# A two-layer hybrid transformer on one core: the experts' output gate computed earlier, and the order of the experts' weight loads

## The chip, the cores and the metric

The kernel runs as one program on one NeuronCore of a Trainium2 chip. The metric is the device time of one execution in microseconds (us). Every weight is read from HBM once per execution; the activations stay on the chip. The engines named below are PE (TensorE, matmuls), PEld (its weight loads, in the records), DVE (VectorE), ACT (ScalarE), POOL (GpSimd) and SP (SyncE, which here only issues weight loads).

## The reference

One sequence of 256 tokens, width 1024, two layers, all in f32:

```
for l in range(DEPTH):                       # DEPTH = 2
    mod = silu(c) @ w_ada[l] + b_ada[l]      # c: (1, 1024), w_ada[l]: (1024, 6144)
    sh1, sc1, g1, sh2, sc2, g2 = split(mod, 6)
    h = rms_norm(x, gain[l, 0]) * (1 + sc1) + sh1
    # four token mixers (NSA, sliding window, MoBA, MLA) read h @ w_in[l]
    mixed = sum_i(sigmoid(G_i h) * (mixer_i @ w_branch[l, i])) @ w_out[l]
    x = x + g1 * mixed
    h2 = rms_norm(x, gain[l, 1]) * (1 + sc2) + sh2
    x = x + g2 * hier_moe(h2, w_coarse, b_coarse, w_fine, b_fine, w13, w2)
```

`hier_moe` picks one of 4 groups and 2 of its 8 experts for each token; an expert is `(silu(a) * b) @ w2[e]` with `a, b = split(x @ w13[e], 2)`, `w13[e]` 1024x512 (2 MB) and `w2[e]` 256x1024 (1 MB). All 32 experts are read in each layer. The part of the change is `g2`, the gate on the experts' output: 1024 columns of `mod`, a product of a vector with a 4 MB slice of `w_ada[l]`.

## The kernel before, in words

**One layer.** A layer has two stages. In the first, the mixers, PE works through a list of *units* (projections, attention, gates, output projection), and beside it a *side list* of smaller units. A written-out string `SEQ[l]` says which list gives the next unit: a letter `a` takes the next one of the side list. The side list holds `ada(l, part)`, the slices of `mod` other than the experts' gate. In the second stage, `experts(l)`, the experts run in eight rounds p = 0..7 of four experts each, an expert's two halves of `w13` first, then its two halves of `w2`.

**The slice of mod.** `ada_pe(l, part)` (L554) makes five units of one slice and a last group. Units 0 to 3 are four matmuls each (32x512, `mm<-ring,cs` or `mm<-pg,cs` in the order; each shows as two records in the trace), each unit with one 1 MB load of `w_ada`. Unit 4, `evac`, copies the sum from PSUM by ACT to a tile `gt` and adds two bias rows by small DMAs on POOL. For part 5 two `rows` units follow, which spread the row over 128 partitions (one matmul and one ACT copy each). In `experts(l)` before, these seven units are called through `filler(n)`: unit 0 ahead of the last part of the router, units 1 to 3 and `evac` between that part and `route`, the two `rows` units in round p = 0 after `first(p, 1)`.

**The route.** `route` is a chain of small DVE instructions on the router's logits; PE continues behind it with short matmuls on `smb` with the constants `tri` and `one_b`, then the seeds (`mm<-pg,K`), the gather of tokens (`at<-pg 128x256`) and `first(0, 0)`, the first expert matmuls.

**The weights.** All weight loads go through SP's one queue in the order of `plan`. A load of 1 MB takes one of 8 slots of `ring`, or (tag "any") two pages of 0.5 MB where no ring slot is free; the halves of `w2`, 0.5 MB each, take one page and never a ring slot. `advance()` walks the plan while the program is built, and stops at the first load that finds no place; `done(key)` gives a place back and calls `advance()` again. On the chip each load waits for the last reader of the place that it takes, and all behind it in the queue wait too. In the plan before, the four loads of part 5 stand behind the loads of `w_out`, and directly ahead of the first `w13`.

In the rows, nearly all engine instructions stand at L253 (a helper that records each), the weight loads at L320 and the router's weights for the next layer at L415 and L416.

Of the kernel before, what the change touches and what calls it, by code (L numbers as in the profile page):

```python
# [49 lines left out]
def shape_constants():  # L50
# [20 lines left out]
    for b, sl in enumerate(_slopes()):  # L71
        for i in range(2):
# [8 lines left out]
SEQ = {0: "u u p u p u p u u u p f p u p f f p A f f q f A A p f f A A r f A N N N . p w f . p p p f . N N b N "  # L81
# [25 lines left out]
SEQ = {l: t.split() for l, t in SEQ.items()}  # L107

KEYS = {0: "in,0,0,1 in,0,0,0 in,0,1,0 in,0,1,1 in,0,2,0 ada,0,3,0 in,0,2,1 ada,0,3,2 ada,0,3,1 ada,0,3,3 "
# [10 lines left out]
KEYS = {l: [tuple(int(f) if f.isdigit() else f for f in k.split(",")) for k in t.split()] for l, t in KEYS.items()}  # L120
KREC = {}
REC = {}
# [136 lines left out]
def kernel(ctx, tc, x_in, c_in, w_ada, b_ada, norm_gain, w_in, qk_gain, cmp_pe, cmp_w1, cmp_w2,  # L259
# [36 lines left out]
    plan, tiles, free = [], {}, {"ring": NRING, "pg": 0}  # L296
    nxt = [0]

    def unit(key, *dmas, tag="ring"):
        plan.append((key, dmas, tag))  # L300

    def advance():
        while nxt[0] < len(plan):
            key, dmas, tag = plan[nxt[0]]
            if tag == "any":
                tag = "ring" if free["ring"] or free["pg"] < 2 else "pg"
            m = 2 if tag == "pg" and len(dmas) == 2 else 1
            if free[tag] < m:
                return
            free[tag] -= m  # L310
            if tag == "ring":
                t = [T_("ring", [128, 2048])]
            else:
                t = [pg([128, 1024]) for _ in range(m)]
            if len(t) == 1 and len(dmas[0]) == 5:
                dmas = [(0, 2048, dmas[0][2], dmas[0][4])]
            for i, d in enumerate(dmas):
                o0, o1, n, src = d[:4]
                d = t[0][:, o0:o1] if m == 1 else t[i]
                nc.sync.dma_start(d.rearrange("p (k n) -> p k n", n=n) if n else d, src)  # L320
            tiles[key] = t[0] if m == 1 else t
            M.t["D"] = max([M.t["D"]] + [M.free(a.tensor.name) for a in t]) + (1.5 if tag == "pg" and m == 1 else 2.9)
            for a in t:
                M.known(a, M.t["D"] + 2.0)
            nxt[0] += 1
# [1062 lines left out]
    def ada(l, part):  # L1388
        how = HOW[l][part]
        return ada_pe(l, part) if how == "p" else ada_v(l, part, how == "g")  # L1390


    def fill_list(l):
# [26 lines left out]
        out = u[0][:4] + [m[1]] + u[0][4:] + u[1][:2] + r[0:1] + u[1][2:4] + r[1:2] + u[1][4:8] + g[0:2]  # L1420
        out += u[2][:4] + r[2:3] + u[2][4:] + g[2:3]
        rbias = router_bias(l)
        if l == 0:
            rest = load_rest()
            side = [(None, lambda: next(rest, None), None, 0)] * LOADN
            side += ada(0, 3) + rbias + ada(0, 2) + ada(0, 4) + [(None, lambda: params(1), None, 0.1)] + ada(1, 1)
            side += [(None, lambda: V.tensor_copy(tri, tri_f), None, 0)]
        else:
            side = ada(1, 4) + ada(1, 3) + rbias + ada(1, 2)
        first = gemm_units(l, 0, CH[0][1], first_fin, ("uh", "ul")) + [(None, lambda: gate_tile(l), None, 0)]  # L1430
        loads = LOADN if l == 0 else 0
        every = (len(base) * LASTS[l] - SIDE[l]) / (len(side) - loads)
# [10 lines left out]
                keys.append(side[n][1][2])  # L1443
                n += 1
        keys += [x_[1][2] for x_ in side[n:]] + [x_[2] for x_ in out]
        return base + out, side, len(base) + 6, keys

    P1 = 2
    P2 = 2
# [8 lines left out]
    LASTS = (0.98, 0.98)  # L1458
    LOADS = 2.0
    LOADN = 8  # L1460
    fills = [fill_list(l) for l in range(DEPTH)]

    def expert(p, b, s):
# [3 lines left out]
    def plan_all():  # L1467
        seen = set()

        def add(key):  # L1470
            if key is not None and key not in seen:
                seen.add(key)
                plan_key(key)

        for k in range(4):
            add(("ada", 0, 1, k))
        for l in range(DEPTH):
            for k in range(2):
                add(("in", l, 0, k))
            for k in range(4):  # L1480
                add(("ada", l, 0, k))
            for key in (KEYS or {}).get(l) or fills[l][3]:
                add(key)
            for key in fills[l][3]:
                add(key)
            KREC[l] = [k for k in dict.fromkeys(fills[l][3]) if k]
            for k in range(4):
                add(("ada", l, 5, k))
            for p in range(NE // 4):
                for b in range(2):  # L1490
                    for hf in range(2):
                        for s in range(2):
                            add(("w13", l, expert(p, b, s), hf))
                for b in range(2):
                    for k in range(2):
                        for s in range(2):
                            add(("w2", l, expert(p, b, s), k))
# [5 lines left out]
    def mixers(l):  # L1503
# [61 lines left out]
            return True  # L1565

        free["pg"] = 0
        R.clear()
        OT.clear()
        M.reset()  # L1570
# [498 lines left out]
                                T.matmul(acc[t][n], st[:, 0, 128 * t:128 * t + 128], y[:, j], start=False, stop=False)  # L2069

    def experts(l):
        units = ada_pe(l, 5)

        def filler(n):
            for _ in range(n):
                units.pop(0)[1]()


        acc = {}

# [2 lines left out]
            for n in range(2):  # L2083
                T.matmul(acc[t][n], ID, X[t][:, 512 * n:512 * n + 512], start=True, stop=False)

        filler(1)
        mm = router_part(l, 3)
        seeds(0)
        rs = rstd_of(H["ss"])
# [11 lines left out]
                c = slice(512 * h, 512 * h + 512)  # L2101
                A.activation(H["hh"][t][:, c], X[t][:, c], AF.Copy, scale=rs[:, t:t + 1])
        mm()
        filler(4)
        most, further, weights = route(l, rs, lo)
        seeds(1)

# [3 lines left out]
        def prep_sel(q):  # L2111
            SEL[q], ST[q] = selection(rk[:, :, 4 * q:4 * q + 4], 4)
            XG[q] = [pg([128, 4, 256]) for _ in range(2)]
# [25 lines left out]
        def second(p, gT):  # L2139
# [12 lines left out]
                        done(("w2", l, expert(p, b, e), k))  # L2152
            return ys

        prep_sel(0)
        most()
        for i in range(1, 4):
# [8 lines left out]
        for p in range(NP):  # L2166
# [12 lines left out]
            h = first_half(h, masks(p)[0])  # L2179
            g = swiglu(first(p, 1), h, masks(p))  # L2180
            if p == 0:
                filler(2)
            if p:
                scatter(acc, ST[(p - 1) // 2][:, (p - 1) % 2], ys, False)
            if nxt:
# [82 lines left out]
```

## Time and profile before

| what | value |
|---|---|
| median of 3 runs | 1033.31 us (1030.22 to 1036.1) |
| the profiled execution's own time | 1038.59 us |
| its span | 1037.0 us |
| PE busy in the span | 982.9 us (95%), 5175 matmuls |
| DVE, ACT, POOL busy | 538.9, 406.5, 134.7 us |
| read from HBM | 335.36 MB |
| layer 0: first expert matmul | 309.26 us |
| layer 1: first expert matmul | 816.17 us |
| last record but the output | 1031.7 us |

The span runs from the first to the last instruction of the profiled execution; the execution's own time is 1.6 us longer, and lies 5.3 us above the median of the runs. All positions below are us from the span's start.

### The profile page before, as it was taken

The numbers are of one execution on the slowest core, as the hardware profiler recorded it, in microseconds if no ns is written. First come the engines' busy times: TensorE is split into PE (matmuls) and PEld (weight loads), VectorE is DVE, ScalarE is ACT, GpSimd is POOL, SyncE is SP. The second block draws the span as 40 slices with busy tenths as digits, with TensorE's granted clock in tenths as the row PEclk, the third lists the DMA queues.
The fourth block names the chain that finished last, engine by engine and source line by source line (L and its number), as shares of the span: only waits on it lengthen the run. The fifth ranks groups of instructions, "written<-read, shape, count | busy, mean of one in ns | idle before, by whom it ended". The sixth has DMA issues, their size and how long they took to land.

```text
span 1037.0 us, 14343 instructions
## 1 busy us (share of the span) xinstructions
PE 982.9 (95%) x5175; PEld 601.1 (58%) x5176; DVE 538.9 (52%) x1237; ACT 406.5 (39%) x997; POOL 134.7 (13%) x271
## 2 busy tenths in 40 slices
PE   5999999999999999998899989999999999999996
PEld 2667777777774444442346857777878444444332
DVE  1667678979772222221156865987785523222112
ACT  1564857674442111110146557677354221111111
POOL 0031346302000000000001341603200000000000
PEclk7999999999999999999999989999999999999999
DMA  9977767478889999999997774566796999999995
GB/s 341 412 238 298 277 205 239 165 250 310 344 326 410 401 356 420 419 418 420 420 408 268 266 299 156 167 222 209 260 395 225 357 390 418 420 420 420 420 420 209
DMA packets 118462, 337.47 MB, mean 325 GB/s; under 512 B 13372, under 2 KB 31084, under 8 KB 118380
## 3 DMA queue, kind: packets, MB, share of 16 engines
q1 hardware_dynamic: 115670, 334.95, 84.3%
q10 hardware_dynamic: 2518, 1.47, 0.5%
q8 instruction: 44, 0.72, 0.3%
q14 instruction: 38, 0.31, 0.1%
q0 software_dynamic: 192, 0.02, 0.0%
HBM read 335.36 MB, written 1.05 MB: 324 GB/s over the span
## 4 chain that ended last, share of the span: by engine, by line
PE 57%; DMA 25%; DVE 8%; ACT 4%; POOL 3%; issue 2%; SPq 0%; ACTq 0%; DVEq 0%; POOLq 0%
PE mm L253 31%; PE at L253 26%; DMA pg<-in_w_dram 12%; DMA ring<-in_w_dram 11%; DVE pg L253 6%; ACT pg L253 3%; POOL sm L253 2%; DMA ring<-in_w_ada_dram 2%; DVE gt L253 1%; POOL pg L253 1%; ACT gt L253 1%; DMA rbs<-in_b_fine_dram 1%; DVE sm L253 1%; DVE smb L253 0%; POOL smb L253 0%
## 5 line engine op out<-in xcount | busy, mean ns | idle before, releaser
L253 PE MATMUL mm<-pg 128*128 128x512 f32 (+4 forms) x1856 | 434.1, 386 | 8.5 <-DVE pg L253 6.3
L253 PEld LDWEIGHTS mm<-pg 128*128 128x128 f32 x1856 | 329.3, 189 | 103.5 <-issue 22.8
L253 PE MATMUL at<-ring,pg 128*64 128x512 f32 (+3 forms) x888 | 239.3, 576 | 14.7 <-DMA ring<-in_w_dram 10.6
L253 DVE TENSOR_TENSOR pg<-ring,pg 128x512 fp32r<-128x512 f32 (+4 forms) x276 | 182.2, 696 | 63.6 <-ACT pg L253 62.8
L253 PE MATMUL at<-pg 128*64 128x512 f32 (+6 forms) x960 | 193.5, 390 | 2.2 <-DVE pg L253 1.1
L253 PEld LDWEIGHTS at<-ring,pg 128*64 128x64 f32 (+2 forms) x888 | 80.7, 139 | 134.0 <-issue 95.1
L253 ACT ACTIVATE pg<-ring 128x512 fp32r<-128x512 f32 (+4 forms) x276 | 148.6, 600 | 10.4 <-PE mm L253 3.6
L253 PEld LDWEIGHTS at<-pg 128*64 128x64 f32 (+3 forms) x960 | 97.4, 161 | 57.2 <-issue 41.2
L253 PE MATMUL at<-pg,gt 128*64 128x512 f32 x512 | 113.4, 595 | 2.7 <-ACT gt L253 2.7
L253 DVE SCALAR_TENSOR_TENSOR gt<-at,sm,gt 128x512 f32<-128x512 f32 x16 | 12.0, 751 | 191.4 <-PE at L253 191.4
L253 ACT ACTIVATE pg<-pg,sm 128x128 f32<-128x128 f32 (+2 forms) x168 | 70.5, 460 | 16.4 <-DVE sm L253 11.8
L253 PEld LDWEIGHTS at<-pg,gt 128*64 128x64 f32 x512 | 35.3, 137 | 68.5 <-issue 62.0
L253 ACT ACTIVATE pg<-at 128x512 f32<-128x512 f32 (+5 forms) x98 | 45.4, 495 | 64.4 <-PE at L253 64.1
L253 DVE SCALAR_TENSOR_TENSOR gt<-at,sm,pg 128x512 f32<-128x512 f32 x32 | 23.9, 748 | 86.4 <-PE at L253 86.4
L253 ACT ACTIVATE pg<-gt 128x512 fp32r<-128x512 f32 x32 | 20.2, 632 | 114.0 <-DVE gt L253 112.5
L253 PE MATMUL at<-K,pg 128*128 128x128 f32 (+1 forms) x356 | 55.3, 285 | 4.2 <-DVE pg L253 1.8
L253 DVE SCALAR_TENSOR_TENSOR pg<-ring,cs,pg 128x1024 f32<-128x1024 f32 x44 | 58.1, 1321 | 0.1
L253 ACT ACTIVATE gt<-mm 128x512 f32<-128x512 f32 x44 | 25.8, 596 | 78.1 <-PE mm L253 76.8
L253 PEld LDWEIGHTS at<-K,pg 128*128 128x128 f32 (+1 forms) x356 | 43.4, 150 | 18.9 <-issue 5.8
L253 ACT ACTIVATE gt<-gt 128x256 f32<-128x256 f32 x16 | 6.7, 419 | 119.1 <-DVE gt L253 119.1
L253 ACT ACTIVATE gt<-at,sm 128x512 f32<-128x512 f32 x16 | 11.0, 689 | 87.4 <-PE at L253 71.9
L253 POOL TENSOR_TENSOR pg<-pg,gt 128x512 f32<-128x512 f32 x16 | 29.6, 1875 | 108.1 <-DVE gt L253 108.1
(166 smaller groups left out, 669.5 us busy)
## 6 DMA issues: line engine op xcount, KB each, us to landing
pg<-in_w_dram SPq DMA_DIRECT2D x202, 512.0 KB, 11.6
ring<-in_w_dram SPq DMA_DIRECT2D x91, 1024.0 KB, 12.7
ring<-in_w_ada_dram SPq DMA_DIRECT2D x45, 1024.0 KB, 8.1
ring<-in_w_in_dram SPq DMA_DIRECT2D x33, 1024.0 KB, 5.0
ring<-in_cmp_w_dram SPq DMA_DIRECT2D x8, 1024.0 KB, 6.8
ring<-in_w_branch_dram SPq DMA_DIRECT2D x8, 1024.0 KB, 4.8
ring<-in_w_out_dram SPq DMA_DIRECT2D x8, 1024.0 KB, 4.9
ring<-in_w_in_dram SPq DMA_DIRECT2D x8, 976.0 KB, 7.6
```

The lines of the kernel that those rows point to most:

```text
L253: return f(*args, **kw)
```

## The change

Three things are edited. **The units**: the first five units of part 5 (four matmul units and `evac`) go to the end of the mixers' side list, and `SEQ` has five more `a` per layer, near the end of each string; the two `rows` units stay in round p = 0 and are taken from `GATE2`; the calls of `filler` ahead of the router's last part and ahead of `route` are gone. **The loads**: the four loads of part 5 stand in `KEYS` ahead of `w_out`'s (in layer 0 ahead of its last three, in layer 1 ahead of all four). **The look-ahead**: while the mixers are built (`look[0] = 16`), a `w2` load that finds no page lets the next `w13` load within 16 places of the plan go ahead of it, when a ring slot is free; from the start of the expert rounds the rule is off again (`look[0] = 0`). No byte and no matmul is added or removed in total.

```diff
-           "in,0,9,1 br,0,2 ada,1,1,0 in,0,10,1 ada,1,1,1 in,0,11,1 ada,1,1,2 ada,1,1,3 br,0,3 in,0,12,1 "
-           "in,0,12,0 out,0,0,1 out,0,1,1 out,0,1,0 ",
+           "in,0,9,1 br,0,2 ada,1,1,0 in,0,10,1 ada,1,1,1 in,0,11,1 ada,1,1,2 ada,1,1,3 br,0,3 "
+           "in,0,12,1 in,0,12,0 ada,0,5,0 ada,0,5,1 ada,0,5,2 ada,0,5,3 out,0,0,1 out,0,1,1 out,0,1,0 ",
...
+    look = [0]
+
     def advance():
         while nxt[0] < len(plan):
             key, dmas, tag = plan[nxt[0]]
@@ -306,7 +311,13 @@
                 tag = "ring" if free["ring"] or free["pg"] < 2 else "pg"
             m = 2 if tag == "pg" and len(dmas) == 2 else 1
             if free[tag] < m:
-                return
+                i = nxt[0]
+                ahead = [j for j in range(i + 1, min(i + 1 + look[0], len(plan)))
+                         if plan[j][0][:2] == ("w13", key[1])] if key[0] == "w2" and free["ring"] else []
+                if not ahead:
+                    return
+                plan.insert(i, plan.pop(ahead[0]))
+                continue
...
+        gate2 = ada_pe(l, 5)
+        GATE2[l] = gate2[5:]
...
-            side += [(None, lambda: V.tensor_copy(tri, tri_f), None, 0)]
+            side += [(None, lambda: V.tensor_copy(tri, tri_f), None, 0)] + gate2[:5]
         else:
-            side = ada(1, 4) + ada(1, 3) + rbias + ada(1, 2)
+            side = ada(1, 4) + ada(1, 3) + rbias + ada(1, 2) + gate2[:5]
...
-            for k in range(4):
-                add(("ada", l, 5, k))
...
+        look[0] = 16
...
-        units = ada_pe(l, 5)
-
-        def filler(n):
-            for _ in range(n):
-                units.pop(0)[1]()
-
...
-        filler(1)
         mm = router_part(l, 3)
...
-        filler(4)
         most, further, weights = route(l, rs, lo)
...
+        look[0] = 0
         prep_sel(0)
...
             if p == 0:
-                filler(2)
+                for u in GATE2.pop(l):
+                    u[1]()
```

How instructions move. First PE in layer 0, near the end of the mixers (`mm<-pg 128x512` and `at<-K,pg` are the output projection and its transposes). Before:

```order
L253 MATMUL mm<-pg 128x512 x12
L253 MATMUL at<-K,gt 128x2 x4
L253 MATMUL mm<-pg 128x512 x6
L253 MATMUL at<-K,pg 128x128 x8
L253 MATMUL mm<-pg 128x512 x30
L253 MATMUL at<-K,pg 128x128 x8
L253 MATMUL mm<-pg 128x512 x24
```

and with the change:

```order
L255 MATMUL at<-K,pg 128x128 x8
L255 MATMUL mm<-pg 128x512 x18
L255 MATMUL mm<-ring,cs 32x512 x4
L255 MATMUL mm<-pg 128x512 x12
L255 MATMUL mm<-ring,cs 32x512 x4
L255 MATMUL at<-K,pg 128x128 x8
L255 MATMUL mm<-ring,cs 32x512 x4
L255 MATMUL mm<-pg 128x512 x12
L255 MATMUL mm<-pg,cs 32x512 x4
L255 MATMUL mm<-pg 128x512 x12
```

The four matmul units of the gate now stand between pieces of the output projection, two ahead of its second group of eight transposes, one directly behind it and one 12 matmuls later. In layer 1 they stand likewise, the first two ahead of the first of these groups.

Second, PE in layer 0 at the router's end (`at<-wr,pg` are the logits, `tri` and `smb` the first matmuls that need the route). Before:

```order
L253 MATMUL at<-wr,pg 128x40 x4
L253 MATMUL mm<-pg,cs 32x512 x4
L253 MATMUL at<-K,pg 128x128 x4
L253 MATMUL mm<-pg,K 128x512 x2
L253 MATMUL at<-wr,pg 128x40 x4
L253 MATMUL mm<-ring,cs 32x512 x12
L253 LDWEIGHTS tri
L253 MATMUL at<-smb,tri 128x16
```

and with the change:

```order
L255 MATMUL at<-wr,pg 128x40 x4
L255 MATMUL at<-K,pg 128x128 x4
L255 MATMUL mm<-pg,K 128x512 x2
L255 MATMUL at<-wr,pg 128x40 x4
L255 LDWEIGHTS tri
L255 MATMUL at<-smb,tri 128x16
```

Between the last logits and the first matmul on the route's result nothing is left on PE. In layer 1 it is the same.

Third, SP's queue in layer 0, from the last loads of `w_out` on (`in_w_dram` are the experts' weights: in `ring` or two pages a half of `w13`, in one page a half of `w2`). Before:

```order
L320 DMA ring<-in_w_out_dram 128x4x512 x3
L320 DMA pg<-in_w_ada_dram 128x1024 x2
L320 DMA ring<-in_w_ada_dram 128x2x1024 x3
L320 DMA pg<-in_w_dram 128x1024 x2
L320 DMA ring<-in_w_dram 128x2x1024 x2
L320 DMA pg<-in_w_dram 128x1024 x4
L320 DMA ring<-in_w_dram 128x2x1024
L320 DMA pg<-in_w_dram 128x1024 x12
L320 DMA ring<-in_w_dram 128x2x1024 x7
L320 DMA pg<-in_w_dram 128x1024 x10
```

and with the change, as far as the ring's eighth expert load and the loads behind it:

```order
L331 DMA pg<-in_w_dram 128x1024 x2
L331 DMA ring<-in_w_dram 128x2x1024
L331 DMA pg<-in_w_dram 128x1024 x2
L331 DMA ring<-in_w_dram 128x2x1024 x2
L331 DMA pg<-in_w_dram 128x1024
L331 DMA ring<-in_w_dram 128x2x1024
L331 DMA pg<-in_w_dram 128x1024 x5
L331 DMA ring<-in_w_dram 128x2x1024
L331 DMA pg<-in_w_dram 128x1024
L331 DMA ring<-in_w_dram 128x2x1024
L331 DMA pg<-in_w_dram 128x1024 x3
L331 DMA ring<-in_w_dram 128x2x1024 x2
```

Ahead of these rows stand, with the change, three `ring` and two `pg` loads of `w_ada`, the three of `w_out`, two pages and two ring loads of expert weights. The ring loads that stood in one row of seven are now spread among the page loads. Ahead of the last row shown, the queue has 8 ring loads and 16 page loads of expert weights; before, ahead of the load that waits for `first(0, 0)` (the sixth of the row of seven), it had 8 and 18.

## Rows read from the trace of the kernel before

**Rows 1.** Chain that ended last, layer 0's experts: start us, us, what

```profile
305.48 44.80 PE at L253 x232
...
401.36 0.75 PE mm L253 x3
402.11 16.45 DMA ring<-in_w_dram
```

**Rows 2.** The same chain, layer 1's experts

```profile
878.60 14.89 DMA ring<-in_w_dram
...
1013.23 3.66 PE at L253 x14
```

**Rows 3.** Stretches: us, busy PE, PEld, DVE, ACT, POOL, clock, DMA share, GB/s

```profile
290.00:300.00 10.00, 10.00 (x76) 8.16 (x74) 4.70 (x19) 4.08 (x13) 0.00 (x0) 1.00 0.87 282
...
340.00:350.00 10.00, 10.00 (x48) 3.16 (x44) 0.00 (x0) 0.69 (x1) 0.00 (x0) 1.00 0.96 375
370.00:380.00 10.00, 10.00 (x59) 5.99 (x56) 2.37 (x5) 1.93 (x4) 0.00 (x0) 1.00 0.81 260
402.00:511.00 109.00, 101.69 (x475) 42.33 (x475) 23.81 (x50) 14.10 (x25) 0.00 (x0) 1.00 1.03 420
...
780.00:790.00 10.00, 9.40 (x66) 8.70 (x65) 5.82 (x13) 4.64 (x14) 0.00 (x0) 1.00 0.56 206
...
879.00:1013.00 134.00, 128.00 (x606) 53.91 (x604) 30.00 (x60) 19.69 (x35) 0.00 (x0) 1.00 1.03 420
```

**Rows 4.** PE in order of time, layer 0: start us, us, what

```profile
271.89 1.03 PE L253 MATMUL at<-K,pg 128*128 128x128 f32 x8
273.90 7.17 PE L253 MATMUL mm<-pg 128*128 128x512 f32 x36 [0.97 <-DVE pg L253]
```

**Rows 5.** PE in order of time, layer 0, from the router's end

```profile
295.99 1.07 PE L253 MATMUL mm<-pg,cs 128*32 128x512 f32 x8
296.99 0.74 PE L253 MATMUL at<-K,pg 128*128 128x128 f32 x4
...
299.28 0.98 PE L253 MATMUL at<-wr,pg 128*128 128x40 f32 x8
300.19 2.78 PE L253 MATMUL mm<-ring,cs 128*32 128x512 f32 x24
303.28 0.18 PE L253 MATMUL at<-smb,tri 128*128 128x16 bf16 x1 [0.30 <-DVE smb L253]
```

**Rows 6.** DVE in order of time, layer 0, ahead of the router's last part

```profile
296.17 0.43 DVE L253 TENSOR_TENSOR pg<-pg,gt 128x256 f32<-128x256 f32 x1
```

**Rows 7.** Chain that ended last, layer 0's route

```profile
300.08 0.48 DVE smb L253 x2
...
302.96 0.27 DVE smb L253
```

**Rows 8.** SP's loads in order of time, layer 0

```profile
257.49 13.14 SPq L320 DMA_DIRECT2D ring<-in_w_dram  x2
...
297.98 5.43 SPq L320 DMA_DIRECT2D ring<-in_w_dram  x5
...
312.94 3.78 SPq L320 DMA_DIRECT2D ring<-in_w_dram  x2
```

**Rows 9.** SP's loads in order of time, layer 1

```profile
781.75 23.30 SPq L320 DMA_DIRECT2D pg<-in_w_dram  x10
805.11 2.10 SPq L320 DMA_DIRECT2D ring<-in_w_dram  x4
...
819.80 0.89 SPq L320 DMA_DIRECT2D ring<-in_w_dram  x2
```

**Rows 10.** Stretches around the start of layer 1 (columns as in rows 3)

```profile
605.00:612.00 7.00, 5.63 (x56) 2.66 (x60) 3.88 (x8) 0.46 (x1) 5.17 (x17) 0.52 0.75 285
272.00:274.00 2.00, 1.02 (x10) 0.79 (x8) 0.84 (x2) 1.47 (x3) 0.00 (x0) 1.00 0.95 379
```

**Rows 11.** PE in order of time, start of layer 1

```profile
606.37 6.44 PE L253 MATMUL at<-ring,pg 128*32 128x256 f32 x64 [3.58 <-POOL pg L253]
```

More of the change, by code (lines that the diff above doesn't have):

```diff
@@ L1445, in fill_list @@
         keys += [x_[1][2] for x_ in side[n:]] + [x_[2] for x_ in out]
-        return base + out, side, len(base) + 6, keys
+        return base + out, side, len(base) + 14, keys
     P1 = 2
@@ L1460 @@
     LOADN = 8
+    GATE2 = {}
     fills = [fill_list(l) for l in range(DEPTH)]
```

42 rows, old and new, of tables (KEYS, SEQ) are left out of this document.

## The prediction

> **What bounds the kernel now.** I read the chain of work that ended last first, to know which resource sets the end of each stage, then the stretches, then PE, DVE and SP in order of time around the place of the change. In layer 0's experts the chain lies on PE from 305.48 with hardly a break (its pieces run on to 401.36 + 0.75 = 402.11) and then passes to DMA [rows 1]; in layer 1 DMA takes over at 878.60 and holds it to 1013.23, where the last expert's matmuls follow [rows 2]. In those DMA stretches 420 GB/s flow without a break, 109 us in layer 0 and 134 us in layer 1 [rows 3]: nothing done in them on PE can matter. Ahead of 402 it is the reverse. PE is busy 10.00 of 10 us, and DMA has holes: 282 GB/s at 290:300, 375 at 340:350, 260 at 370:380, 206 at 780:790 [rows 3]. In these holes loads wait for places that PE has still to give back. So each layer's experts have two phases: one bound by PE, in which places come free at PE's pace, and one bound by DMA, which ends at the time when the bytes left at its start are through. A microsecond put on PE ahead of the switch delays the places, so the loads, so the end.
>
> Around the change, what hides the gate's matmuls now? In layer 0 the last logits end at 300.19; then PE runs 2.78 us of `mm<-ring,cs` (units 1 to 3), then the first matmul on the route's result comes at 303.28 after 0.30 us of idle [rows 5]. The DVE chain of the route, from 300.08 to 302.96 + 0.27 = 303.23, is what that matmul waits for [rows 7]. So three of the four units cost nothing today: the route hides them. Only unit 0 stands in the open, 295.99 to 296.99 [rows 5].
>
> **The change part by part.**
>
> *Units 0 to 3, put among the mixers.* One unit is 2.78 / 3 = 0.93 us [rows 5]; four are 3.7 us. Their new neighbours are the output projection's matmuls, where PE is busy all but 0.97 us: after the transposes ending at 272.9 it waited 0.97 us for DVE and then began at 273.90 [rows 4]. The order puts unit 2 exactly there, and two more units ahead give DVE time, so I take the whole 0.97 back. PE: +3.7 − 0.97 = +2.7 in layer 0. In layer 1 the first two units stand ahead of the corresponding transposes and none directly behind them: I take nothing back there, +3.7.
>
> *Unit 0, taken away from the router's end.* The transposes at 296.99 came behind it [rows 5], but the DVE result that they read was ready only at 296.17 + 0.43 = 296.60 [rows 6]. So at most 296.99 − 296.60 = 0.4 us comes back, not 1.07. From there to `tri` the DVE chain decides, and the other three units' absence saves nothing: PE waits 3.0 us (300.26 to 303.28) where it waited 0.30. Cover gone in the mixers, cover unused in the route: that is the heart of it. First expert matmul: +2.7 − 0.4 = **+2.3 us** in layer 0, +3.7 − 0.4 = +3.3 in layer 1.
>
> *`evac`, the two bias DMAs and the `rows` units.* The ACT copy from PSUM moves into the output projection, where ACT is busy about 4 of 10 us (the nearest stretch has 4.08 [rows 3]); the bias DMAs and the `rows` units stay where they were in the order of their engines. Zero; if the PSUM bank of the gate's sum is missed by the output projection, one wait of some tenths, which I leave in the range.
>
> *The four loads of part 5 ahead of `w_out`.* The same bytes in another order. They push `w_out` back by at most 4 MB, 4.2 MB / 420 GB/s = 10 us; by my reading of the queue `w_out` still lands in time. Zero, with a late `w_out` in the range.
>
> *The look-ahead, and the ring's places free earlier.* Before, the ring loads of `w13` in the row of seven went out only from 297.98, behind twelve page loads; five of them were out by 303.4, and the sixth waited for `first(0, 0)`, at 312.94 [rows 8]. With the change ring loads go ahead of page loads, and part 5 holds no place of the ring then. By the order, up to the first load that waits for `first(0, 0)`, 8 ring and 16 page loads are out: 16 MB; before it was 8 and 18, 17 MB. So the bytes start earlier, but the store is full at the same event and is not larger. Three ring loads and six page loads or so are out by 271 (the second ring load went at 270.6 [rows 8]), and what is left, about 13 MB, takes 13.6 / 0.42 = 32 us: done at about 305 to 308. Then DMA idles until PE releases a place: 312.94 + 2.3 = 315.2. The hole of 290:300 is filled and a new one of some 8 us opens at 307. PE never waited for a weight in this phase (rows 1 has one piece of 44.80 us), so an earlier landing shortens nothing. From there on the loads follow PE's releases and are late by what PE is late. Layer 0's switch and end: **+2.3 us**.
>
> In layer 1 the queue before stood longest on page loads, ten in 23.3 us from 781.75, with ring loads of `w13` behind them until 805.11, and the next waited for the first expert matmuls until 819.80 [rows 9]. Here the head start is larger, and following the queue's waits place by place I get later loads of round 2 that are late by some 1.6 to 2.2 us where PE is late by 3.3. I take **+2.0 us**.
>
> Sum without any other effect: 2.3 + 2.0 = +4.3 us.
>
> *The clock in the new idle time.* PE's granted clock is 1.00 nearly everywhere. At the start of layer 1, after an idle of 3.58 us [rows 11], it shows 0.52 over 605 to 612 [rows 10], which is the 1.2 GHz level: about 7 us at half rate, of which some 1.1 us lay in the idle itself, so about 3 us of work lost. After an idle of 0.97 us it stays at 1.00 [rows 4, 10]. The new idle of 3.0 us in each layer lies between, nearest to the 3.58 that fell. I give each layer a chance of 0.55; the likeliest count is one of two. One fall costs about +3 us: half of 6.8 us, less the rest of the idle. It strikes the seeds, the gather and the first expert matmuls, all PE-bound, so it passes on to the releases.
>
> The Trainium skill, "TensorE: Matmul & The Clock Gate", section "HAM oscillation — how this bites in real kernels", describes just that: PE waits between bursts, the clock goes to half, and work after the wait pays for it. Rows 10 and 11 agree with it at 3.58 us; by that rule taken alone both layers would fall, and the sum would be 4.3 + 6 = 10.3 us, by the row at 0.97 alone 4.3 us.
>
> Likeliest: 4.3 + 3 = +7.3 us. The profiled execution took 1038.59, 5.3 above the median of the runs; these terms are differences, so I put them on the median: 1033.3 + 7.3 = 1040.6, say **1041 us**.
>
> **The rivals.**
>
> *The head start counts.* DMA's holes ahead of the switch are real: at 290:300, (420 − 282) / 420 of 10 us is 3.3 us, at 780:790 5.1 us, and the neighbours of the latter are alike. If loads out early are not held by `first(0, 0)`, because more places are free than the order of the program suggests, the DMA phase begins with fewer bytes left. 5 us a layer less the PE shift of 2.3 and 3.3: about −4 to −10, or 1023 to 1029. It decides if the row of loads that waits for `first(0, 0)` has more than 17 MB ahead of it. Against it: the order has 16. Chance 0.17.
>
> *Moved, and neutral.* The mixers absorb the units: waits of PE for DVE that a busy PE hides in the trace shrink as in [rows 4], and the clock stays. Some +1 to +3 us: 1034 to 1037. Chance 0.12.
>
> *The sum without a clock fall.* 3.0 us of idle is not enough in either layer: +4.3, 1037.6. Chance 0.2.
>
> *One fall*, the forecast: 1039 to 1043. Chance 0.31.
>
> *Both fall, or a late `w_out` on top.* 4.3 + 6 = 10.3: 1043 to 1047. Chance 0.2.
>
> **How the numbers follow.** 0.5% is 5.2 us, about what a measurement of this kernel can tell from no change: faster means below 1028, slower above 1038.5. Faster is the first rival: 0.17. Same is the neutral case, the sum without a fall, and a small tail of the forecast's case: 0.33. Slower: 0.50. The range leaves out 0.1 below and as much above: 1029 to 1047; the forecast's own is 1036 to 1044.
>
> **What would show it.** PE in order of time at the router's end: a wait of about 3 us ahead of `tri` in both layers, and the granted clock of the next 10 us, 1.00 or about 0.6. The output projection: three of four units in the open, no wait of 0.97 us in layer 0. First expert matmul of layer 0 at about 311.6, of layer 1 some 6 us or more later than 816.2. Stretches: 270:307 near 420 GB/s, then a hole until about 315. The switch to DMA at the same bytes, later by PE's shift. I would be wrong if that hole is not there, if loads beyond the ring's eighth go out ahead of the first expert matmuls, or if the last load of layer 0 lands earlier than before.

## The result, and the profile after

The changed kernel is slower: 1044.4 us (median of 4 runs, 1041.04 to 1046.5) against 1034.7 us for the kernel before on the same occasion (4 runs), a ratio of 1.0105 with a 95% interval of 1.0081 to 1.0128, so +9.7 us. In a second comparison (6 runs against 17) it was 1.0117, interval 1.0097 to 1.0136, +12.6 us. The forecast was 1041, +7.3 us on the median that it started from, with a range to 1047.

The profiled execution after spans 1039.4 us, only 2.4 more than that of before. That difference of two single executions misleads, and the rows show why. Layer 1 began in the kernel before with the idle of 3.58 us and seven microseconds at half clock of [rows 10, 11]; in the twelve other executions profiled for this study the granted clock stays at 1.00 there, and between the same two DVE instructions (602.05 to 617.37 before, 603.88 to 614.45 after) the kernel before took 4.8 us more. And that execution was 3.2 us later already at a matmul ahead of all that the change moves (257.04 against 253.84). So I compare stage by stage.

PE in order of time in the changed kernel, layer 0, answers to [rows 4]:

```profile
266.03 1.07 PE L255 MATMUL mm<-ring,cs 128*32 128x512 f32 x8
267.03 3.02 PE L255 MATMUL mm<-pg 128*128 128x512 f32 x12
269.98 1.06 PE L255 MATMUL mm<-ring,cs 128*32 128x512 f32 x8
270.98 1.09 PE L255 MATMUL at<-K,pg 128*128 128x128 f32 x8
272.00 1.06 PE L255 MATMUL mm<-ring,cs 128*32 128x512 f32 x8
273.05 3.02 PE L255 MATMUL mm<-pg 128*128 128x512 f32 x12
```

The third unit begins at 272.00, where PE stood waiting before, and no idle is left in front of 273.05: the 0.97 us came back. But each unit takes 1.00 to 1.05 us from its start to the next row's start, not 0.93.

PE in order of time at the router's end, layer 0 and then layer 1, answers to [rows 5]:

```profile
299.20 0.98 PE L255 MATMUL at<-wr,pg 128*128 128x40 f32 x8
303.19 0.18 PE L255 MATMUL at<-smb,tri 128*128 128x16 bf16 x1 [3.01 <-DVE smb L255]
...
303.43 1.96 PE L255 MATMUL mm<-pg,K 128*128 128x512 f32 x4
...
804.15 0.98 PE L255 MATMUL at<-wr,pg 128*128 128x40 f32 x8
808.14 0.19 PE L255 MATMUL at<-smb,tri 128*128 128x16 bf16 x1 [3.02 <-DVE smb L255]
...
808.38 3.76 PE L255 MATMUL mm<-pg,K 128*128 128x512 f32 x4
```

PE now waits 3.0 us for the route in both layers. The matmuls `mm<-pg,K` behind it take 1.96 us in layer 0, as before, and 3.76 us in layer 1: there they run at half rate.

Stretches (columns as in rows 3) answer to [rows 3]:

```profile
290.00:300.00 10.00, 9.65 (x71) 8.51 (x69) 5.07 (x21) 4.00 (x13) 0.00 (x0) 1.00 1.03 422
305.00:312.00 7.00, 7.00 (x47) 5.03 (x48) 5.99 (x23) 1.94 (x4) 0.00 (x0) 1.00 0.01 4
312.00:320.00 8.00, 8.00 (x42) 3.12 (x40) 2.39 (x14) 1.51 (x3) 0.00 (x0) 1.00 0.67 233
340.00:350.00 10.00, 10.00 (x48) 3.16 (x44) 0.00 (x0) 0.69 (x1) 0.00 (x0) 1.00 1.03 422
370.00:380.00 10.00, 10.00 (x60) 6.01 (x54) 2.46 (x5) 1.93 (x4) 0.00 (x0) 1.00 0.89 283
805.00:812.00 7.00, 3.98 (x12) 1.79 (x12) 6.69 (x33) 2.47 (x6) 0.40 (x2) 0.62 0.00 0
812.00:820.00 8.00, 8.00 (x49) 5.61 (x49) 4.41 (x19) 1.97 (x4) 0.00 (x0) 0.91 0.01 3
```

The hole of DMA at 290:300 is filled (282 before, 422 now). A new one stands at 305:312 with 4 GB/s. In layer 1 it is longer: nothing from 805 to 820. SP's loads in order of time say what they wait for, and answer to [rows 8, 9]:

```profile
292.15 4.05 SPq L331 DMA_DIRECT2D pg<-in_w_dram  x3
312.86 3.80 SPq L331 DMA_DIRECT2D ring<-in_w_dram  x2
...
792.88 3.95 SPq L331 DMA_DIRECT2D pg<-in_w_dram  x4
820.21 0.38 SPq L331 DMA_DIRECT2D ring<-in_w_dram  x1
```

The queue is through at 296, stops, and goes on at 312.86, when the first expert matmuls give a ring slot back, as `first(0, 0)` did at 312.94 before. All weights that found a place came earlier; the next did not.

The chain that ended last answers to [rows 1, 2] (layer 0, then layer 1; start us, us, what):

```profile
377.21 2.37 PE at L255 x20
...
379.88 13.60 DMA ring<-in_w_dram
```

```profile
910.70 22.95 PE at L255 x116
...
933.66 14.89 DMA ring<-in_w_dram
```

In layer 0 DMA becomes the bound at 379.9, where it did at 402.1 (381.6 in units_only): it has more to catch up. In layer 1 PE stays the bound until 933.6, where it passed on at 878.6: there DMA is ahead.

### The profile page after: what moved, and what is told of

Same layout as the page of the kernel before. It is cut to its first block, busy times and chain, and to the rows that moved or that the text cites. A ratio compares the mean times of both kernels' runs of the same rounds, so it can differ in the third digit from the quotient of the medians.

```text
span 1039.4 us, 14342 instructions
## 1 busy us (share of the span) xinstructions
PE 985.0 (95%) x5175; PEld 601.8 (58%) x5176; DVE 539.1 (52%) x1237; ACT 404.7 (39%) x997; POOL 133.4 (13%) x271
## 3 DMA queue, kind: packets, MB, share of 16 engines
HBM read 335.36 MB, written 1.05 MB: 324 GB/s over the span
## 4 chain that ended last, share of the span: by engine, by line
PE 60%; DMA 22%; DVE 10%; ACT 4%; POOL 2%; issue 2%; SPq 0%; ACTq 0%; DVEq 0%; POOLq 0%
PE mm L255 32%; PE at L255 27%; DMA pg<-in_w_dram 11%; DMA ring<-in_w_dram 9%; DVE pg L255 7%; ACT pg L255 3%; DVE gt L255 2%; POOL sm L255 1%; DMA ring<-in_w_ada_dram 1%; POOL pg L255 1%; ACT gt L255 1%; DVE sm L255 1%; DMA rbs<-in_b_fine_dram 1%; DVE smb L255 0%; POOL smb L255 0%
## 5 line engine op out<-in xcount | busy, mean ns | idle before, releaser
L255 PE MATMUL at<-ring,pg 128*64 128x512 f32 (+2 forms) x912 | 249.1, 562 | 12.9 <-DMA ring<-in_w_dram 10.8
L255 DVE TENSOR_TENSOR pg<-ring,pg 128x512 fp32r<-128x512 f32 (+4 forms) x268 | 179.4, 704 | 58.2 <-ACT pg L255 57.4
L255 PE MATMUL at<-pg 128*64 128x512 f32 (+6 forms) x936 | 198.0, 387 | 2.2 <-DVE pg L255 1.1
L255 PEld LDWEIGHTS at<-ring,pg 128*64 128x64 f32 (+2 forms) x912 | 83.7, 135 | 128.2 <-issue 89.3
L255 ACT ACTIVATE pg<-ring 128x512 fp32r<-128x512 f32 (+4 forms) x268 | 145.9, 604 | 11.3 <-DVE pg L255 4.2
L255 ACT ACTIVATE pg<-pg,sm 128x128 f32<-128x128 f32 (+2 forms) x168 | 70.1, 457 | 17.5 <-DVE sm L255 12.8
```

The source lines that it names most:

```text
L255: return f(*args, **kw)
```

## The stages of all kernels

From PE's records I took the start of the same matmul in every profiled execution: one of the mixers ahead of all moved units (257.04 in layer 0 and 754.93 in layer 1 of the kernel before), the first on `tri`, one of the first expert matmuls (309.26 and 816.17), and the first on the last expert weights (510.88 and 1013.23). (In layer 1 the first expert matmuls read pages and start earlier than 816.17, which the table ahead of the prediction calls the first; 816.17 is the first of a row that reads the ring, and the same matmul stands at 820.02 after. So "gather" holds some 3.5 us of expert matmuls in layer 1.) The differences are stage durations in us, free of what happened earlier in that execution. "sum" adds up the six differences to the kernel before; "measured" is its median time less that of the kernel before in the same comparison (without the run of 5532 us that units_only had). before_p4 and after_p4 are not in it: their last loads go out in another order, and the last landmark isn't the same.

```
              layer 0: mixers gather experts | layer 1: mixers gather experts |   sum  measured
before               46.2    6.0   201.6     |      51.8     9.4   197.1     |
after                49.4    6.0   204.0     |      56.2    11.9   196.0     | +11.4   +9.7
after_again          49.3    7.6   204.5     |      56.2    12.1   196.0     | +13.6  +12.6
units_only           49.4    7.6   203.6     |      56.1    11.0   197.2     | +12.8  +14.2
no_look              49.4    7.6   203.8     |      56.2    12.2   196.0     | +13.1  +10.6
cover                49.3    6.0   203.8     |      56.2     9.4   196.1     |  +8.7   +7.6
two_units            47.0    6.0   203.8     |      53.8     9.4   196.1     |  +4.0   +4.0
after_hold           49.4    7.6   204.1     |      56.2    12.0   193.2     | +10.4   +9.8
look_only            46.3    6.0   202.3     |      51.8     9.4   196.7     |  +0.4   -1.0
loads_only           46.2    6.0   200.7     |      51.8     9.4   194.4     |  -3.6   -3.5
loads_hold           46.2    6.0   200.1     |      51.8     9.4   193.2     |  -5.4   -3.5
```

The six stages account for the measured differences within 2.6 us, and mostly within 2. Three things are to be seen. The mixers' stages depend on the units alone (+3.2 and +4.4 with four, +0.8 and +2.0 with two). The gather's stages (`tri` to the first expert matmuls) are longer only where PE idles 3.0 us ahead. The experts' stage of layer 0 is longer by 2.0 to 2.9 us in every kernel with moved units, units_only with its loads in the old order among them, and is not where the units stay at the route (-1.5 to +0.7); that of layer 1 is shorter where the gate's loads go out early (-1.0 to -3.9) and as before in units_only.

## The experiments

**The units alone (units_only).** The loads of part 5 behind `w_out` as before, no look-ahead:

```diff
-            "in,0,12,1 in,0,12,0 ada,0,5,0 ada,0,5,1 ada,0,5,2 ada,0,5,3 out,0,0,1 out,0,1,1 out,0,1,0 ",
+            "in,0,12,1 in,0,12,0 out,0,0,1 out,0,1,1 out,0,1,0 ",
...
-        look[0] = 16
+        look[0] = 0
```

> The gate's units among the mixers, but its loads behind w_out as before and no look-ahead. Theory S (PE shift and store): units cost 3 to 5 us of PE per layer, and the ring and pages hold 16 MB (layer 0) and 17 MB (layer 1) ahead of the first load that waits for the first expert matmuls, where before they held 17 and 17; a missing MB costs 2.5 us of DMA. Expected: +8 to +11 us, nearly all of the whole change. Theory L (the loads' new order is what costs): 0 to +3 us, since the order is nearly that of before.

1.0136 (1.0109 to 1.0163; one run of 5532 us is not in it): no less than the whole change, whose two intervals overlap with this one. The units' move by itself costs all of the loss. The loads' new order can't be its cause.

**Without the look-ahead (no_look).** `look[0] = 0` in the changed kernel.

> The whole change without the look-ahead. Theory S: the store is 16 and 15 MB as with the whole change, and PE is shifted alike: +9 to +11 us, as the whole change. Theory L, with the look-ahead at fault: 0 to +4 us. If the look-ahead helps by its early loads, this one is slower than the whole change by 2 us or more.

1.0101 (1.0081 to 1.0121), like the whole change: beside the moved units the look-ahead is worth nothing that can be measured.

**The look-ahead alone (look_only).** The kernel before with the new `advance()` and `look[0] = 16` for the mixers.

> The kernel before with the look-ahead alone; units and the gate's loads stay. Theory S: PE is where it was and the store holds 17 and 17 MB, only earlier: -1 to +1 us, although DMA's hole at 290:300 is filled. Theory L (early loads open a hole ahead of the first expert matmuls, and that costs): +4 to +8 us. If a head start counts by itself: -4 us or more.

0.9984 (0.9969 to 1.0): nothing, or a little gain.

**The loads alone (loads_only).** Look-ahead and the new `KEYS`; the units stay at the route.

> The kernel before with the look-ahead and the gate's loads ahead of w_out; the units stay at the route. Theory S: PE is where it was, the store holds 17 MB in layer 0 and 16 in layer 1: 0 to +2.5 us. Theory L: +5 to +10 us, nearly all of the whole change.

0.9968 (0.9953 to 0.9984), −3.5 us: outside of what either theory gave. The early loads are a gain where the units stay hidden; the stages put it in the experts, −0.9 and −2.7 us. The rival of the head start was right on the sign.

**The changed kernel again (after_again).**

> The changed kernel once more, beside the others on the same chip: +8 to +11 us by its first timing. Its profile is a second execution: if the granted clock after the idle of 3.0 us ahead of tri falls in one layer and not in the other by chance, the layer may be another one this time, or both, or none; if the fall belongs to layer 1's surroundings, it is layer 1 again.

1.0117 (1.0097 to 1.0136). This time the clock fell in both layers. Stretches of 293:312 and 800:818 in this execution (columns as in rows 3):

```profile
293.00:312.00 19.00, 15.64 (x99) 12.85 (x99) 12.50 (x54) 7.50 (x21) 0.40 (x2) 0.91 0.77 315
800.00:818.00 18.00, 14.64 (x88) 11.31 (x87) 11.99 (x53) 6.84 (x20) 0.40 (x2) 0.86 0.42 170
```

**The cover put back (cover).** In `experts(l)` of the changed kernel:

```diff
         mm()
+        p_ = mmb()
+        for j in range(12):
+            T.matmul(p_[32 * (j % 4):32 * (j % 4) + 32], cs[:, j % 8:j % 8 + 1].to_broadcast([128, 32]),
+                     X[0][:, 0:512], start=True, stop=True)
         most, further, weights = route(l, rs, lo)
```

> The changed kernel with 12 more strip matmuls (32x512, 2.8 us) on the token tile, between the last logits and the route's first matmul; nobody reads their result, the output is the same. They fill PE's idle of 3.0 us as the gate's units did. Clock theory: the granted clock stays 1.00 behind the route in both layers, and the time is 2 to 3 us below the changed kernel's (one fall of 1.9 us in layer 1 or more saved). Without a clock effect: the same as the changed kernel within 1 us.

1.008 (1.0062 to 1.0099), 5 us less than the changed kernel beside it (1039.79 against 1044.81), though PE does 12 matmuls more in each layer. PE in order of time and the same stretches:

```profile
298.94 2.78 PE L255 MATMUL mm<-pg,cs 128*32 128x512 f32 x24
302.02 0.18 PE L255 MATMUL at<-smb,tri 128*128 128x16 bf16 x1 [0.30 <-DVE smb L255]
...
302.26 1.96 PE L255 MATMUL mm<-pg,K 128*128 128x512 f32 x4
```

```profile
293.00:312.00 19.00, 18.36 (x121) 11.38 (x122) 14.98 (x68) 6.71 (x17) 0.40 (x2) 1.00 0.54 219
800.00:818.00 18.00, 17.35 (x110) 9.99 (x111) 14.95 (x69) 6.82 (x17) 0.40 (x2) 1.00 0.06 24
```

The idle is 0.30 us again, the clock 1.00 in both layers, `mm<-pg,K` takes 1.96 us. What remains, +7.6 us, is the change without its clock effect. Idle time of PE that costs nothing by itself cost about 4 us by what followed (1.6 + 2.7 in the stages against after_again).

**Two units instead of four (two_units).** The other two and `evac` stay between the last logits and the route:

```diff
-        GATE2[l] = gate2[5:]
+        GATE2[l] = gate2[2:]
...
-            side = ada(1, 4) + ada(1, 3) + rbias + ada(1, 2) + gate2[:5]
+            side = ada(1, 4) + ada(1, 3) + rbias + ada(1, 2) + gate2[:2]
...
         mm()
+        for _ in range(3):
+            GATE2[l].pop(0)[1]()
```

(and the same in layer 0, and three `a` less in each `SEQ`)

> The changed kernel with only two of the four matmul units among the mixers; the other two and evac stay between the last logits and the route, so PE's idle there is about 1.2 us instead of 3.0. PE's stages: mixers of layer 0 +1.0 (the second unit stands in the DVE wait of 0.97 us), of layer 1 +2.4, where the whole change has +3.6 and +4.9; granted clock 1.00 behind both routes. With the loads as in the whole change: +2 to +5 us against before, less than half of the changed kernel's +11. If the loads' part of the change were what costs: +8 or more.

1.0043 (1.0027 to 1.0059), +4.0 us. PE in order of time, layer 0:

```profile
299.15 1.04 PE L255 MATMUL mm<-pg,cs 128*32 128x512 f32 x8
301.35 0.18 PE L255 MATMUL at<-smb,tri 128*128 128x16 bf16 x1 [1.16 <-DVE smb L255]
```

An idle of 1.16 us left the clock alone in both layers. The loss is about half of cover's +7.6 us, which pays for no fall of the clock either, and a third to two fifths of the whole change's.

**More pages (before_p4, after_p4).** `P4_ = (4, 4)` instead of `(0, 0)`: the plan may give out four pages more; the pool of pages itself stays at 29.

> The kernel before with the same four more pages: 18 MB and 18.5 MB ahead of the first load that waits for the first expert matmuls, where it has 17 and 17. Theory S: -3 to -6 us against the kernel before, if the pages are not missed by the experts' own tiles. If the store does not set the end: 0.

> The changed kernel with four more pages for the experts' weights (P4 = 4, 4). The loads ahead of the first that waits for the first expert matmuls then make 18 MB in layer 0 and 17 in layer 1, where the change has 16 and 15. Theory S: a MB is 2.5 us of DMA at 420 GB/s, so about 4 to 9 us less than the changed kernel, 0 to +5 against the kernel before. If only PE's shift counts: no change against the changed kernel, +8 to +11.

1.0029 (1.0016 to 1.0042) and 1.0161 (1.0142 to 1.018): both slower than without. The store can't be enlarged in this way. The loads go out into pages that the experts' own tiles hold, and wait there at the queue's head: in layer 1 eight page loads take 17.15 us from 819.51, where eight took 7.93 us in the kernel before. One stretch of 15 us each from before_p4, layer 0 and layer 1, 10 us after the first expert matmuls:

```profile
318.52:333.52 15.00, 15.00 (x80) 7.26 (x78) 3.05 (x6) 4.03 (x8) 0.00 (x0) 1.00 1.03 418
825.45:840.45 15.00, 15.00 (x80) 7.30 (x78) 5.07 (x9) 4.66 (x9) 0.00 (x0) 1.00 0.65 241
```

In layer 1 241 GB/s, where 379 flowed in the same stretch (826.17 to 841.17) of the kernel before. That a MB more ahead of the first expert matmuls is worth 2.5 us, as I had expected, these two don't show; they don't refute it either, since the pages weren't free.

**Loads with a page ahead of waiting ring loads (after_hold, loads_hold).** In `advance()`, with `hold[0]` true while `first(0, 0)` is placed:

```diff
+            if hold[0] and tag == "ring":
+                ahead = [j for j in range(nxt[0] + 1, len(plan)) if plan[j][0][:2] == ("w2", key[1])] if free["pg"] else []
+                if not ahead:
+                    return
+                plan.insert(nxt[0], plan.pop(ahead[0]))
+                continue
```

> The changed kernel, and in round p = 0 a first half of w13 that would take a ring slot waits in the plan until the matmuls of first(0, 0) have been placed, while w2 loads that have a page go ahead of it. By the queue's waits 17.5 MB (layer 0) and 16.5 MB (layer 1) are then out ahead of the first load that waits for the first expert matmuls, where the change has 16 and 15, without a page more. If loads with a free page that stand behind a waiting ring load are what the changed kernel's DMA idle of 6.4 us after layer 0's first expert matmul costs: 2 to 5 us less than the changed kernel (+7 to +10 against before). If the queue's order is not what counts, since later loads then wait for the same matmuls: within 1 us of the changed kernel, +10 to +12.

> The kernel before with the gate's loads early, the look-ahead, and the same rule in round p = 0; the units at the route. 17.5 and 16.5 MB ahead of the first waiting load instead of 17 and 16. Against loads_only (-3.3 us against before): 1 to 2.5 us less by the first theory, so -4 to -6 against before; the same (-2 to -4) by the second.

1.0095 (1.0074 to 1.0117) and 0.9964 (0.9948 to 0.998). Layer 0 gained nothing in after_hold and layer 1 gained 2.8 us in its experts' stage. Why not in layer 0? Its stretches 0 to 10 and 10 to 25 us after the first expert matmuls:

```profile
312.79:322.79 10.00, 10.00 (x51) 3.88 (x52) 4.89 (x26) 1.51 (x3) 0.00 (x0) 1.00 0.47 154
322.79:337.79 15.00, 15.00 (x80) 7.26 (x78) 3.05 (x6) 4.03 (x8) 0.00 (x0) 1.00 0.79 300
```

The bytes came earlier, and the queue stood idle again in the next 15 us: the idle moved. loads_hold is, with loads_only, the fastest kernel of the study, 3.5 us below the kernel before; the two can't be told apart.

## Why the prediction was right, and where not

The direction and the main mechanism were right, and the size was too small: +7.3 us was forecast, +9.7 and +12.6 were measured. Units that the route hid now stand in the open in the mixers, and PE waits 3.0 us ahead of `tri` instead. Two terms were mis-sized, the unit among the mixers and the clock, and one step failed: that layer 0's experts end late by PE's shift alone.

*The units in the mixers.* Forecast for the first expert matmul ahead of any clock effect: +2.3 and +3.3 us. Measured: +3.2 and +4.4. The wait of 0.97 us did come back in layer 0 and not in layer 1, as forecast. Mis-sized is the unit: 2.78 / 3 = 0.93 us holds for three in a row; alone among other matmuls it took 1.00 to 1.05, and the matmuls around it were longer too. In layer 1 the first 12 matmuls behind a group of transposes take 3.37 us to the start of the next row, where before 30 took 6.94, so 2.8 for 12. Before, and then after:

```profile
768.32 7.11 PE L253 MATMUL mm<-pg 128*128 128x512 f32 x30
775.26 1.03 PE L253 MATMUL at<-K,pg 128*128 128x128 f32 x8
```

```profile
767.40 3.44 PE L255 MATMUL mm<-pg 128*128 128x512 f32 x12
770.77 1.06 PE L255 MATMUL mm<-ring,cs 128*32 128x512 f32 x8
```

(The 0.4 us that unit 0's absence at the router's end gives back is in both numbers.) Per unit 1.1 to 1.2 us would have been right. The records one by one say where that goes: from start to start a matmul of such a row takes 0.23 us, the last ahead of a unit 0.32, the last of the unit's records 0.52 where the step inside the unit is 0.43, and the first behind it 0.34. So the change from one shape to the other, there and back, lengthens the neighbours. In layer 1's row of 12 one more step is 0.52 us long, with 0.13 us of idle; the two_units and units_only profiles have it too, and its cause stays open.

*The store and the new hole.* Right in every step but the last. 16 MB ahead of the first waiting load, DMA idle from about 305 to 315, that load released by `first(0, 0)`: all as forecast. The last step, that layer 0's end is late by PE's shift alone, failed: the experts' stage grew by 2.4 us, and the switch to DMA came at 379.88 instead of somewhat behind 402.11. Stretches from the first expert matmul: 10 us and the whole stage, of before, layer 0:

```profile
309.26:319.26 10.00, 10.00 (x51) 3.88 (x52) 4.88 (x26) 1.52 (x3) 0.00 (x0) 1.00 1.00 399
309.26:510.88 201.62, 194.31 (x932) 81.48 (x931) 48.06 (x113) 29.98 (x54) 0.00 (x0) 1.00 1.01 408
```

and of after:

```profile
309.17:319.17 10.00, 10.00 (x51) 3.88 (x52) 4.88 (x26) 1.51 (x3) 0.00 (x0) 1.00 0.45 153
309.17:513.22 204.05, 196.47 (x932) 82.58 (x931) 48.07 (x113) 29.90 (x54) 0.00 (x0) 1.00 0.99 396
```

In the stage 201.62 us × 408 GB/s = 82.26 MB flowed before and 204.05 × 396 = 80.80 MB after: 1.46 MB less was left at its start, 3.5 us at 420 GB/s. But in the first 10 us DMA lost (420 − 399) / 420, 0.5 us, before and 6.4 us after. 5.9 − 3.5 is the 2.4 that the stage grew by. It is not the early loads that do this. The same stretches in units_only, whose loads stand in the old order, and then in loads_only, whose loads are early:

```profile
311.16:321.16 10.00, 10.00 (x51) 3.89 (x52) 4.90 (x26) 1.51 (x3) 0.00 (x0) 1.00 0.44 156
311.16:514.74 203.58, 195.23 (x931) 81.49 (x930) 48.10 (x113) 29.91 (x54) 0.00 (x0) 1.00 0.99 397
```

```profile
307.04:317.04 10.00, 10.00 (x51) 3.88 (x52) 4.88 (x26) 1.51 (x3) 0.00 (x0) 1.00 1.00 378
307.04:507.78 200.74, 194.31 (x932) 80.81 (x931) 48.09 (x113) 29.90 (x54) 0.00 (x0) 1.00 1.02 409
```

units_only has the hole, 156 GB/s, and 80.8 MB in the stage; loads_only has neither, 378 GB/s and 82.1 MB. So the hole belongs to the units' move. What goes with it is the store, which the forecast had counted and then given no price: SP's queue has put out 16 MB of expert weights ahead of the load that goes on 3.7 us behind layer 0's first expert matmul in after, units_only, no_look, cover and two_units, 17 MB in before, look_only and loads_only, and 17.5 in loads_hold. A MB less is 2.5 us at 420 GB/s, and those five kernels' stage grew by 2.0 to 2.9 us, two_units with a PE shift of only 0.8 us among them. That fits, but isn't shown to be the cause: after_hold had 17.5 MB ahead, and its stage grew by 2.5 us all the same. In layer 1 I forecast that the experts' stage gives 1.3 us back (+2.0 against PE's +3.3); it gave back 1.1.

*The clock.* I forecast one fall of 3 us out of two, chance 0.55 each. In the six profiled executions with the 3.0 us of idle, layer 1 fell six times (1.6 to 2.8 us, gather 11.0 to 12.2 against 9.4) and layer 0 five times (1.6, in after_p4 2.5); with 0.30 or 1.16 us of idle (cover, two_units), not once. One fall came in the first profile of the changed kernel alone, two in the other five. So the rival of two falls was the true one, at about 4 us instead of 6. The Trainium skill, "TensorE: Matmul & The Clock Gate", in "HAM oscillation — how this bites in real kernels", says that waits between bursts of matmuls bring the clock down; 11 falls behind 12 idles of 3.0 us agree with it, and behind 1.16 us no fall is seen. That both layers would fall by it was a step of the forecast's own: the section doesn't say that an idle of 3.0 us is enough.

*In sum.* Without the clock I had +4.3, and cover shows +7.6 by its time and +8.7 by its stages: the units in the mixers cost 2.0 us more than forecast in the two layers (0.9 and 1.1), and layer 0's experts 2.2 us in cover, which I had at nothing. The clock was +3 in the forecast and about +4. Faster by the head start was right in the one part of the change that stood alone (−3.5 us in loads_only), and was outweighed.

## What to carry to other kernels

Work that hides in another engine's latency is free where it stands; look for what hides it before moving it, and price it in its new place among its new neighbours, not in a row of its own kind. An idle stretch of TensorE left behind isn't free either: here 3.0 us of it brought the clock down and a filler of useless matmuls won 5 us. Count what a load queue can put out ahead of the first load that waits, and give a difference there a price: here 16 MB instead of 17 went with 2.0 to 2.9 us. Compare bytes and DMA's lost time over the whole stage, and test each part of a change alone: here the early loads were a gain of 3.5 us where the units stayed, inside a change that lost 10, and the hole that looked like their work was there without them.

## What the runs showed of the hardware that I had not expected

How far the clock falls behind the same idle time varies from execution to execution: behind 3.01 us in layer 0 the granted clock of 293:312 was 1.00 in the first profile of the changed kernel and 0.91 in the second. And the start of layer 1, where no kernel of the study differs but in what came before, took 4.8 us more in the one profile of the kernel before than in all others, by the idle of 3.58 us and the half clock behind it. In look_only PE stood idle at the same place for 2.77 us, and the granted clock of 600:608 stayed at 1.00; in before_p4 it was 0.76 in 505:512, around an idle of 2.58 us near the end of layer 0's experts. The shorter of the two idles was followed by a fall, the longer wasn't.
